# Gates' one-hots with two tokens side by side, eight tokens a step, in a two-layer transformer kernel

## The chip, the cores and the metric

The kernel runs on one core of a Trainium2 chip. The core has TensorE (PE: matmuls, and PEld: its weight loads), VectorE (DVE), ScalarE (ACT), GpSimd (POOL) and SyncE (SP), on whose queue the DMA transfers of this kernel are issued. The metric is the device time of one execution in microseconds; lower is better.

## The reference, cut to what matters

Two blocks of a transformer over 256 tokens of width 1024, in float32. Each block has a token mixer and ends with product-key experts (PEER); between the two comes cross attention to a memory. The change lies in the experts' part, which runs twice, once for each block:

```python
q = (xt @ w_pq).reshape(T, PEER_HEADS, 2, PEER_QDIM // 2)
s = jnp.einsum('thpd,hpnd->thpn', q, subkeys)          # 8 heads, 2 halves, 128 keys
top_s, top_i = lax.top_k(s, 16)
cand_s = top_s[:, :, 0, :, None] + top_s[:, :, 1, None, :]
best_s, best_pos = lax.top_k(cand_s, 16)               # over 256 candidates
expert = 128 * (first index) + (second index)          # one of 16384
gate = jax.nn.softmax(best_s, axis=-1)
act = jax.nn.gelu(jnp.einsum('thkd,td->thk', peer_u[eb], xb)) * gb
out = jnp.einsum('thk,thkd->td', act, peer_v[eb])
```

So each token selects 8 x 16 = 128 experts, each given by two indices from 0 to 127, and each has a gate.

## The kernel before, in words

The experts are not gathered. The kernel computes the first layer for all 16384 experts and all 256 tokens, multiplies by a dense table of gates that is zero where an expert was not selected, and multiplies by the whole second table. Every large float32 matmul is made of three of exact halves (`mm3`, line 292: high x high, high x low, low x high). A tile of weights, 128 x 1024, comes by DMA into one of four `raw` buffers; ScalarE rounds it to its high half `wh` and VectorE subtracts to get the low half `wl` (`split`, line 273; `weight`, line 282), each in two pieces of 512 columns, of which seven are held.

**The gates' table.** For one token t the table over first index i and second index j is a product of two one-hot matrices over the 128 selections: the sum over selections of gate x [second index = j] x [first index = i]. In `gates` (line 1141) this is done for four tokens at a time. `ids` holds the two indices of every selection (partition) and token in 16 bits, `gate` the gate times 2^15 in two 16-bit parts. VectorE makes `hot[:, 0:2]`, the one-hots of both indices (line 1148, 128 x 1024 elements: two indices, 128 values, four tokens), and then `hot[:, 2:4]`, the second one-hot times each part of the gate (line 1151, again 1024 elements). Both are in one `work` tile of 4 KB a partition; there are two, used by turns. TensorE then makes, for each token, two matmuls into the psum tile `pg` (line 1156): 128 stationary columns, a gate part's one-hot of that token, and 128 moving columns, the first index's one-hot of that token. As the token is the last axis of `hot`, these columns are taken with a step of four elements. ScalarE copies `pg` in two halves into `S` (line 1160), and after each 16 tokens two DMAs write `S` to the table `gd` in memory (line 1164). 256 tokens are 64 steps, and 512 `pg` matmuls in each of the two expert layers.

**What it is mixed with.** `up` (line 1169) is the first expert layer: for each of the 128 tiles of the table, a load, a split and 24 matmuls into `ph` (line 298) with 256 moving columns, and a gelu on ScalarE into `hid` after every second tile. `mix` (line 200) puts the steps of the selection and of the gates (`chain`, line 1216) between those of the table (at most 94 tiles, `AHEAD`) in one order: a tile of the table gives a credit of `UP` = 1.4, and each yield of the gates uses up `GATES` = 0.5 (after the one-hots) or 0.3 (after the copies). The order of the instructions on each engine is then settled by a scheduler on that order. Waits follow from the data. SP's queue has the loads and the writes in one order.

**What follows.** After the gates, `fetch` (line 1196) reads back the first part of the table, `gt`, `prep` (line 1201) multiplies it into `hid` on VectorE (line 1209) and splits the product into `dah` and `dal`, and TensorE begins the second layer, `acc` (line 1265), by turns with the rest of `up`. Large buffers come from a pool of 33 places of 4 KB a partition (`big`, `NBIG`): here four of the normalized input (`pxh`, `pxl`), four of scores (`S`), two `work`, and one of `hid` for four tiles of the table.

Of the kernel before, what the change touches and what calls it, by code (L numbers as in the profile page):

```python
# [27 lines left out]
# pairs (a, b) of ranks that can be among the 16 best sums of two descending lists of 16: (a + 1) * (b + 1) <= 16, in  # L28
# the order of a * 16 + b; runs of equal length: first a, how many, length
RUNS = [(0, 1, 16), (1, 1, 8), (2, 1, 5), (3, 1, 4), (4, 1, 3), (5, 3, 2), (8, 8, 1)]  # L30
NC = 50
# blocks of q (0-3), k and v of the gated delta rule, in the order of their use
# [3 lines left out]
# ---------------------------------------------------------------- host layout  # L36
def _cols(w):
    """[K, C] -> [C/128, 128 p, K/128, 128 c]: one stationary tile per 128 columns."""
    k, c = w.shape
    return np.ascontiguousarray(w.reshape(k // 128, 128, c // 128, 128).transpose(2, 1, 0, 3))  # L40


def _rows(w):
    """[K, 512] -> [K/256, 128 p, 2, 512]: moving tiles, two blocks of 128 rows each."""
    k, c = w.shape
    return np.ascontiguousarray(w.reshape(k // 256, 2, 128, c).transpose(0, 2, 1, 3))


def _vec(v):
    """[n*128] -> [128, n]"""  # L50
    return np.ascontiguousarray(v.reshape(-1, 128).T)
# [107 lines left out]
# ---------------------------------------------------------------- the program  # L159
class Vec:  # L160
    """[128, n, 256] kept as tiles of four blocks"""
# [8 lines left out]
class Blocks:  # L170
    """[128, 1024] kept as two halves; [k] is the k-th block of 128 columns"""
# [18 lines left out]
def weave(a, b):  # L190
    """steps of a and b by turns"""
    for _ in a:
        yield _
        v = next(b, None)
        if v is not None:
            yield v
    yield from b


def mix(a, b):  # L200
    """Two programs in one order. A step yields the vector engine's time that it takes, less what it leaves
    while the tensor engine is busy with it; a runs on what b leaves."""
# [16 lines left out]
class Norm:  # L219
    """x * g in exact halves (act), and the tokens' 1 / rms apart from it: rc with tokens on partitions, rb as rows.  # L220
    The latter are made when they are first asked for."""
# [12 lines left out]
class Net:  # L234
# [21 lines left out]
    # -- tiles  # L256
# [15 lines left out]
    # -- exact halves of float32: hi rounded to the tensor engine's float32r, lo the rest  # L272
# [9 lines left out]
    def weight(self, ap):  # L282
        """a tile [128, 1024] from memory: its exact parts, each as two halves"""
# [8 lines left out]
    def mm3(self, out, pairs):  # L292
        """sum of (ah+al)^T (bh+bl), without al^T bl, which is under float32's last place"""
# [7 lines left out]
    def dense(self, w, n, act, use):  # L301
        """w: tiles of 128 columns with K = 1024; use(pair, psum[128 c, 2 * 256 t])"""
# [11 lines left out]
    def dense_half(self, w, n, act, use):  # L314
        """w: tiles of two blocks of 128 columns with K = 512"""
# [10 lines left out]
    def dense_tok(self, w, act, use):  # L326
        """tokens on partitions: out[t, 512]; w: four moving tiles of two blocks of 128 rows; use(th, psum)"""
# [17 lines left out]
    def rsqrt(self, y, v, name):  # L345
        """y = v ** -0.5 for v > 0 on a few columns: a first value from the exponent, three Newton steps"""
# [14 lines left out]
    def spread(self, cols, n, out=None):  # L361
        """cols [128 t, n] -> the columns as rows on every partition: psum tiles of four [128, 128 t] each"""
# [12 lines left out]
    def begin(self, x, g, name, stats=True):  # L375
        """the norm of x[k] [128, 256] times g [128, 8], whose pairs of blocks are yet to be fed"""
# [51 lines left out]
    def colsum(self, ps, c, n, x):  # L428
        """ps[:, c] of n columns: the sums of x [128, 128 t] over its partitions"""
# [7 lines left out]
    def copies(self, v, N, scale=1.0):  # L437
        """use() that keeps pairs of column tiles in a Vec, times the tokens' 1 / rms"""
# [25 lines left out]
    def tables(self, which):  # L464
        """the activation tables that the calls of fn() after this one use, loaded after those before it are done"""
# [18 lines left out]
    # ------------------------------------------------------------ block 1, token mixer  # L484
    def sb_attention(self, qk, v, o):
        """stick-breaking; qk: Vec of 8 (4 of q / 8, 4 of k), two heads each; v [t][128, 512]; o: exact halves"""
# [4 lines left out]
        # scores, keys on partitions: of the first 128 keys all queries, of the others the last 128  # L491
# [17 lines left out]
        # softplus, which is zero where masked, and its sums over a key and those after it  # L509
# [24 lines left out]
    def gdn(self, pads, z, ba, out, ready):  # L534
        """gated delta rule; pads: 4 tiles [128, 3, 259] of q, k, v with three columns of zeros first;
        z [128 t, 2, 512]; ba [128 t, 2, 8] (b, then a); out: exact halves, Vecs of 4. ready: names of the blocks
        of pads, of ba and of z as they get there"""
# [17 lines left out]
        # beta, g, and the cumulative sums of g within chunks of 64  # L555
# [22 lines left out]
        gf = g.rearrange("p h c -> p (h c)")  # pack = 2 * head + half  # L578
# [13 lines left out]
        # l2 norms over the head's 128 partitions: k now, q with the output  # L592
# [18 lines left out]
        dm = self.big("dm", (8, 128))   # exp(gc_i - gc_j), i on partitions  # L611
        dt = self.big("dt", (8, 128))   # the same with j on partitions
        eg = self.big("eg", (8, 128))   # exp(gc) on every partition
# [8 lines left out]
        # of the differences d = gc_free - gc_partition only the signs that a causal pair can have  # L622
# [8 lines left out]
        # A, and q k^T with m on partitions  # L631
# [13 lines left out]
        # (I + A)^-1 by blocks of doubling size; Tm the inverse, P its transpose  # L645
# [11 lines left out]
        for s in (2, 4, 8, 16, 32):  # L657
# [25 lines left out]
            if s == 2:  # L683
                # meanwhile k and v with tokens on partitions, and q exp(gc)
# [14 lines left out]
        # u [c, dv] and w^T [dk, c]  # L699
# [11 lines left out]
        # the scan over chunks  # L711
# [38 lines left out]
    def head_out(self, po, th, z, g, out, rq=None, half=False):  # L750
        """the exact halves of rmsnorm(po * rq) * z * g for the heads' [128 t, 128], transposed; half: with z / 2"""
# [31 lines left out]
    def branches(self, gates, wa, oa, wb, ob, wout, N):  # L783
        """N: the norm of the new x.  x += (sigmoid(ga) * (oa @ wa) + sigmoid(gb) * (ob @ wb)) @ wout; gates: Vec of 16;
        sigmoid(y) = (tanh(y / 2) + 1) / 2"""
# [27 lines left out]
    def add_x(self, N):  # L813
        """use() that adds to x and feeds x's next norm"""
# [75 lines left out]
    # ------------------------------------------------------------ cross attention  # L890
# [23 lines left out]
    def patterns(self):  # L914
        """constants of the experts' selection, in 16 bits, which hold them"""
        nc = self.nc
        self.iota4 = self.sm("iota4", 512, F16).rearrange("p (i t) -> p i t", t=4)
        nc.vector.tensor_copy(self.iota4, self.c("iota").unsqueeze(2).broadcast_to([128, 128, 4]))
# [5 lines left out]
    def cross(self, N, kv):  # L924
# [54 lines left out]
        # the values of the last two heads, while the tensor engine has little else to do  # L979
# [10 lines left out]
    # ------------------------------------------------------------ product-key experts  # L990
    def peer(self, N, g, wpq, sub, shared, u, v, gelu, final):
        """returns psum tiles acc[t half][d half] of [128 t, 512] with x plus the experts' sums, and the tile of the
        final gain in rows"""
# [13 lines left out]
        # scores of half the heads and half the tokens each; later the gates on their way to memory  # L1007
# [133 lines left out]
        def gates():  # L1141
            for t0 in range(0, T, 4):
# [19 lines left out]
                if t0 % 16 == 12:  # L1162
                    for i in range(2):
                        nc.sync.dma_start(gd[t0 // 16, :, 64 * i:64 * i + 64, :], gs[i])
# [403 lines left out]
```

## Time and profile before

| | us |
|---|---|
| median of 3 runs | 2252.29 |
| lowest and highest run | 2251.95, 2252.83 |
| span of the profiled execution, first to last instruction | 2251.2 |
| VectorE busy in it | 1643.0 |
| ScalarE busy in it | 1229.7 |

Of the profiled execution the span is what the profile gives as its own time. The views below come from this one execution. In a view of groups a line is: line of the kernel, engine, operation, output<-input, shapes, xcount | busy us, mean ns of one | idle time of the engine just before them, and what ended it. Where a view gives instructions in order of time, neighbours of one line are drawn together; then the second number is the time from the first one's start to the last one's end. Matmuls are pipelined, so a matmul's duration is longer than the step from one to the next.

### The profile page before, as it was taken

The numbers are of one execution on the slowest core, as the hardware profiler recorded it, in microseconds if no ns is written. First come the engines' busy times: TensorE is split into PE (matmuls) and PEld (weight loads), VectorE is DVE, ScalarE is ACT, GpSimd is POOL, SyncE is SP. The second block draws the span as 40 slices with busy tenths as digits, with TensorE's granted clock in tenths as the row PEclk, the third lists the DMA queues.
The fourth block names the chain that finished last, engine by engine and source line by source line (L and its number), as shares of the span: only waits on it lengthen the run. The fifth ranks groups of instructions, "written<-read, shape, count | busy, mean of one in ns | idle before, by whom it ended". The sixth has DMA issues, their size and how long they took to land.

```text
span 2251.2 us, 40741 instructions
## 1 busy us (share of the span) xinstructions
PE 2230.4 (99%) x15268; PEld 2035.2 (90%) x15268; DVE 1643.0 (73%) x3568; ACT 1229.7 (55%) x2237; POOL 1.8 (0%) x12
## 2 busy tenths in 40 slices
PE   8999999999999999999999999999999999999998
PEld 8899899999999999888887899999999999988886
DVE  8776776989778656687446668998887765598544
ACT  6463455656555555565446545655655555566443
POOL 0000000000000000000000000000000000000000
PEclk9999999999999999999999999999999999999999
DMA  6442445455666767787555445455566766698653
GB/s 232 139 150 85 132 150 178 161 189 178 208 231 216 243 206 221 232 288 251 188 188 189 143 132 186 156 192 186 202 217 213 247 216 207 214 297 262 200 190 125
DMA packets 178681, 441.14 MB, mean 196 GB/s; under 512 B 13602, under 2 KB 79266, under 8 KB 178484
## 3 DMA queue, kind: packets, MB, share of 16 engines
q1 hardware_dynamic: 177764, 437.11, 59.3%
q8 instruction: 120, 1.97, 0.4%
q10 hardware_dynamic: 720, 1.44, 0.2%
q14 instruction: 77, 0.63, 0.1%
HBM read 403.89 MB, written 34.60 MB: 195 GB/s over the span
## 4 chain that ended last, share of the span: by engine, by line
PE 95%; DVE 3%; ACT 1%; issue 1%; DMA 0%; ACTq 0%
PE ph L298 32%; PE acc L1265 32%; PE mm L298 17%; PE pg L1156 5%; PE mm L339 3%; DVE wl L275 1%; PE psc L1027 1%; ACT wh L274 0%; PE px L665 0%; PE pp L673 0%; PE cs L937 0%; PE pt L679 0%; PE cpo L963 0%; PE acc L1243 0%; PE spread L371 0%
## 5 line engine op out<-in xcount | busy, mean ns | idle before, releaser
L274 ACT ACTIVATE wh<-raw 128x512 fp32r<-128x512 f32 x1388 | 866.6, 630 | 853.5 <-PE ph L298 308.4
L275 DVE TENSOR_TENSOR wl<-raw,wh 128x512 fp32r<-128x512 f32 x1388 | 944.9, 688 | 483.4 <-ACT wh L274 477.2
L298 PE MATMUL ph<-pxh,wh 128*128 128x256 f32 x2048 | 579.4, 283 | 0.0
L298 PE MATMUL ph<-pxh,wl 128*128 128x256 f32 x2048 | 571.9, 279 | 0.0
L298 PE MATMUL ph<-pxl,wh 128*128 128x256 f32 x2048 | 571.4, 279 | 0.0
L1265 PE MATMUL acc<-wh,dah 128*128 128x512 f32 x1024 | 405.5, 396 | 0.0
L1265 PE MATMUL acc<-wh,dal 128*128 128x512 f32 x1024 | 405.0, 396 | 0.0
L1265 PE MATMUL acc<-wl,dah 128*128 128x512 f32 x1024 | 405.0, 396 | 0.0
L298 PEld LDWEIGHTS ph<-pxh,wh 128*128 128x128 f32 x2048 | 386.5, 189 | 3.1
L298 PEld LDWEIGHTS ph<-pxl,wh 128*128 128x128 f32 x2048 | 385.5, 188 | 3.2
L298 PEld LDWEIGHTS ph<-pxh,wl 128*128 128x128 f32 x2048 | 384.8, 188 | 0.0
L1265 PEld LDWEIGHTS acc<-wh,dal 128*128 128x128 f32 x1024 | 192.3, 188 | 46.6
L1265 PEld LDWEIGHTS acc<-wh,dah 128*128 128x128 f32 x1024 | 192.4, 188 | 43.0
L1265 PEld LDWEIGHTS acc<-wl,dah 128*128 128x128 f32 x1024 | 192.4, 188 | 42.9
L298 PE MATMUL mm<-xnh,wh 128*128 128x256 f32 x496 | 142.7, 288 | 8.9 <-ACT wh L274 8.1
L298 PE MATMUL mm<-xnh,wl 128*128 128x256 f32 x496 | 141.4, 285 | 0.0
L298 PE MATMUL mm<-xnl,wh 128*128 128x256 f32 x496 | 140.7, 284 | 0.0
L1156 PE MATMUL pg<-work 128*128 128x128 f16 x1024 | 133.3, 297 | 0.0
L1156 PEld LDWEIGHTS <-work 128*128 128x128 f16 x1024 | 110.3, 118 | 4.5
L1209 DVE TENSOR_TENSOR hid<-hid,gt 128x512 f32<-128x512 f32 x128 | 86.0, 688 | 35.9 <-DMA gt<-gd 35.2
L274 ACT ACTIVATE dah<-hid 128x512 fp32r<-128x512 f32 x128 | 76.3, 621 | 61.9 <-DVE hid L1209 60.9
L298 PEld LDWEIGHTS mm<-xnh,wh 128*128 128x128 f32 x496 | 95.2, 192 | 11.2 <-ACT wh L274 8.1
(443 smaller groups left out, 2825.7 us busy)
## 6 DMA issues: line engine op xcount, KB each, us to landing
raw<-in_u_dram SPq DMA_DIRECT2D x256, 512.0 KB, 3.6
raw<-in_v_dram SPq DMA_DIRECT2D x256, 512.0 KB, 3.9
gd<-S SPq DMA_DIRECT2D x64, 512.0 KB, 4.1
gt<-gd SPq DMA_DIRECT2D x64, 512.0 KB, 5.8
raw<-in_w_gate_dram SPq DMA_DIRECT2D x32, 512.0 KB, 3.5
raw<-in_w_pq_dram SPq DMA_DIRECT2D x32, 512.0 KB, 3.5
raw<-in_w_g_dram SPq DMA_DIRECT2D x12, 512.0 KB, 4.7
raw<-in_w_qk_dram SPq DMA_DIRECT2D x8, 512.0 KB, 3.5
```

Source lines behind the costliest of these rows:

```text
L274: self.nc.scalar.activation(hi, src, AF.Copy)
L275: self.nc.vector.tensor_tensor(lo, src, hi.bitcast(F32), ALU.subtract)
L298: self.nc.tensor.matmul(out, l, r, start=i == 0, stop=i == n - 1)
L339: nc.tensor.matmul(ps[th], l, r, start=k == 0 and j == 0, stop=k == 7 and j == 2)
L1027: nc.tensor.matmul(pz[:, p * 128:p * 128 + 128], qf[:, p * 256 + th * 128:p * 256 + th * 128 + 128], key(h, p), start=True, stop=True)
L1156: nc.tensor.matmul(pg[:, t * 128:t * 128 + 128], hot[:, c, :, t], hot[:, 0, :, t], start=c == 2, stop=c == 3)
L1209: tt(hv, hv, gv, ALU.mult)
L1265: nc.tensor.matmul(acc[th][dh], l[:, n, sl], r.half[dh], start=i0 + n == 0 and j == 0, stop=i0 + n == 127 and j == 2)
```

## The change

One-hots are made for eight tokens at a time, as four pairs (`b`) of two tokens (`t`), with the two tokens of a pair side by side: the layout is (pair, index, value, token in pair) where it was (index, value, token). `ids` is kept in that order, and `iota4` becomes `iota2`. The one-hots of both indices of eight tokens are one VectorE instruction on 2048 elements and fill a whole `work` tile; the products with the gate's parts are two instructions on 1024 elements each: the second part goes into half of a new tile, `hots`, taken once from the pool of large buffers, and the first part into the place of the second index's one-hot. The matmuls are the same in number and size; their columns are taken with a step of two elements. The eviction of each four tokens is as before. The yields are 0.5, 0.5, 0.3 and 0.3 for eight tokens, and the write to memory comes after the last of them. The other lines of the diff take away comments and docstrings, which leaves the line numbers nearly as they were.

```diff
     def patterns(self):
-        self.iota4 = self.sm("iota4", 512, F16).rearrange("p (i t) -> p i t", t=4)
-        nc.vector.tensor_copy(self.iota4, self.c("iota").unsqueeze(2).broadcast_to([128, 128, 4]))
+        self.iota2 = self.sm("iota2", 256, F16).rearrange("p (i t) -> p i t", t=2)
+        nc.vector.tensor_copy(self.iota2, self.c("iota").unsqueeze(2).broadcast_to([128, 128, 2]))
...
-        ids = self.sm("ids", 512, F16).rearrange("p (c t) -> p c t", c=2)
+        ids = self.sm("ids", 512, F16).rearrange("p (b c t) -> p b c t", c=2, t=2)
...
-                nc.vector.tensor_copy(ids[:, :, th * 128:th * 128 + 128],
-                                      pt[:, 0:256].rearrange("p (c t) -> p c t", c=2))
+                nc.vector.tensor_copy(ids[:, 64 * th:64 * th + 64].rearrange("p b c t -> p c b t"),
+                                      pt[:, 0:256].rearrange("p (c b t) -> p c b t", c=2, t=2))
...
         def gates():
-            for t0 in range(0, T, 4):
+            spare = self.big("hots").bitcast(F16).rearrange("p (n b i t) -> p n b i t", n=2, b=4, t=2)
+            for t0 in range(0, T, 8):
                 if t0 % 16 == 0:
                     gs = [st[t0 // 16 % 2, i].rearrange("p a t -> p (a t)").rearrange("p (i t) -> p i t", t=16)
                           for i in range(2)]
-                # one-hots of the first index; of the second, times each part of the gate
-                hot = work[t0 // 4 % 2].bitcast(F16).rearrange("p (c i t) -> p c i t", c=4, t=4)
-                tt(hot[:, 0:2], self.iota4.unsqueeze(1).broadcast_to([128, 2, 128, 4]),
-                   ids[:, :, t0:t0 + 4].unsqueeze(2).broadcast_to([128, 2, 128, 4]), ALU.is_equal)
+
+                hot = work[t0 // 8 % 2].bitcast(F16).rearrange("p (b c i t) -> p b c i t", b=4, c=2, t=2)
+                part = [hot[:, :, 1], spare[:, t0 // 8 % 2]]
+                tt(hot.rearrange("p b c i t -> p (b c) i t"), self.iota2.unsqueeze(1).broadcast_to([128, 8, 128, 2]),
+                   ids[:, t0 // 2:t0 // 2 + 4].rearrange("p b c t -> p (b c) t").unsqueeze(2).broadcast_to(
+                       [128, 8, 128, 2]), ALU.is_equal)
                 yield self.GATES[0]
-                tt(hot[:, 2:4], hot[:, 1:2].broadcast_to([128, 2, 128, 4]),
-                   gate[:, :, t0:t0 + 4].unsqueeze(2).broadcast_to([128, 2, 128, 4]), ALU.mult)
-                pg = self.ac("pg")
-                for t in range(4):
-                    for c in (2, 3):
-                        nc.tensor.matmul(pg[:, t * 128:t * 128 + 128], hot[:, c, :, t], hot[:, 0, :, t],
-                                         start=c == 2, stop=c == 3)
-                pv = pg.rearrange("p (t i) -> p i t", t=4)
-                for i in range(2):
-                    nc.scalar.activation(gs[i][:, :, t0 % 16:t0 % 16 + 4], pv[:, 64 * i:64 * i + 64, :], AF.Copy,
-                                         scale=1 / GATE)
-                if t0 % 16 == 12:
+                yield self.GATES[0]
+                for c in (1, 0):
+                    tt(part[c], hot[:, :, 1], gate[:, c, t0:t0 + 8].rearrange("p (b t) -> p b t", t=2).unsqueeze(
+                        2).broadcast_to([128, 4, 128, 2]), ALU.mult)
+                for q in range(2):
+                    pg = self.ac("pg")
+                    for t in range(4):
+                        b, e = 2 * q + t // 2, t % 2
+                        for c in range(2):
+                            nc.tensor.matmul(pg[:, t * 128:t * 128 + 128], part[c][:, b, :, e], hot[:, b, 0, :, e],
+                                             start=c == 0, stop=c == 1)
+                    pv = pg.rearrange("p (t i) -> p i t", t=4)
+                    s0 = t0 % 16 + 4 * q
+                    for i in range(2):
+                        nc.scalar.activation(gs[i][:, :, s0:s0 + 4], pv[:, 64 * i:64 * i + 64, :], AF.Copy,
+                                             scale=1 / GATE)
+                    yield self.GATES[1]
+                if t0 % 16 == 8:
                     for i in range(2):
                         nc.sync.dma_start(gd[t0 // 16, :, 64 * i:64 * i + 64, :], gs[i])
-                yield self.GATES[1]
```

## Rows read from the trace of the kernel before

**Rows 1.** The page, part 1: the span; busy us, share of the span, instructions.
```profile
span 2251.2 us, 40741 instructions
...
PE 2230.4 (99%) x15268; PEld 2035.2 (90%) x15268; DVE 1643.0 (73%) x3568; ACT 1229.7 (55%) x2237; POOL 1.8 (0%) x12
```

**Rows 2.** The page, part 4: the chain that ended last, by line, shares of the span.
```profile
PE ph L298 32%; PE acc L1265 32%; PE mm L298 17%; PE pg L1156 5%; PE mm L339 3%; DVE wl L275 1%; PE psc L1027 1%; ACT wh L274 0%; PE px L665 0%; PE pp L673 0%; PE cs L937 0%; PE pt L679 0%; PE cpo L963 0%; PE acc L1243 0%; PE spread L371 0%
```

**Rows 3.** Table by stretch (header line: the columns): both gates' stretches, a later one.
```profile
core 0: us, PE busy (x) PEld busy (x) DVE busy (x) ACT busy (x) POOL busy (x), PEclk, DMA share, GB/s
577.36:739.52 162.16, 162.16 (x1378) 159.88 (x1377) 128.53 (x198) 95.64 (x217) 0.00 (x0) 1.00 0.62 216
1609.20:1771.50 162.30, 162.30 (x1380) 160.00 (x1379) 128.70 (x198) 95.65 (x217) 0.00 (x0) 1.00 0.62 216
...
1900.00:2100.00 200.00, 200.00 (x1043) 169.41 (x1042) 151.47 (x241) 114.97 (x198) 0.00 (x0) 1.00 0.78 250
```

**Rows 4.** Groups of the first gates' stretch: shapes, xcount | busy us, mean ns | idle.
```profile
L298 PE MATMUL ph<-pxh,wh 128*128 128x256 f32 x288 | 83.8, 291 | 0.0
...
L1156 PE MATMUL pg<-work 128*128 128x128 f16 x512 | 66.6, 297 | 0.0
...
L275 DVE TENSOR_TENSOR wl<-raw,wh 128x512 fp32r<-128x512 f32 x74 | 51.3, 693 | 32.1 <-ACT wh L274 30.4
```

**Rows 5.** Instructions in order of time, one table tile into `pg`: start us, us, engine.
```profile
602.36 0.28 PE L298 MATMUL ph<-pxh,wl 128*128 128x256 f32 x1
...
602.71 0.28 PE L298 MATMUL ph<-pxh,wl 128*128 128x256 f32 x1
...
602.83 2.05 PE L1156 MATMUL pg<-work 128*128 128x128 f16 x16
...
604.59 0.21 PEld L298 LDWEIGHTS ph<-pxh,wh 128*128 128x128 f32 x1
```

**Rows 6.** The same view of TensorE, `acc` matmuls after the stretch.
```profile
764.81 0.39 PE L1265 MATMUL acc<-wh,dah 128*128 128x512 f32 x1
...
766.44 0.40 PE L1265 MATMUL acc<-wl,dah 128*128 128x512 f32 x1
```

**Rows 7.** Groups by form, whole span: two matmuls, then weight loads.
```profile
L1027 PE MATMUL psc<-sub,pq 128*128 128x128 f32 x128 | 17.2, 274 | 0.0
...
L937 PE MATMUL cs<-ckT,cxq 128*128 128x256 f32 x32 | 7.9, 389 | 0.0
...
L298 PEld LDWEIGHTS ph<-pxl,wh 128*128 128x128 f32 x2048 | 385.5, 188 | 3.2
...
L1156 PEld LDWEIGHTS <-work 128*128 128x128 f16 x1024 | 110.3, 118 | 4.5
...
L1438 PEld LDWEIGHTS glo<-gstate,gq 128*64 128x64 f32 x32 | 3.1, 135 | 2.6 <-issue 1.2 <-DVE gstate L1432 0.4
```

**Rows 8.** Instructions in order of time, TensorE: the scores of one head.
```profile
497.40 1.05 PE L1027 MATMUL psc<-sub,pq 128*128 128x128 f32 x8
```

**Rows 9.** Groups by form on VectorE, whole span.
```profile
L275 DVE TENSOR_TENSOR wl<-raw,wh 128x512 fp32r<-128x512 f32 x1388 | 944.9, 688 | 483.4 <-ACT wh L274 477.2 <-PE mm L298 1.0
...
L1151 DVE TENSOR_TENSOR work<-work,gate 128x1024 f16<-128x1024 f16 x128 | 83.5, 686 | 0.7
...
L1113 DVE TENSOR_TENSOR work<-work,tf 128x1024 bf16<-128x1024 bf16 x8 | 9.7, 1216 | 0.0
```

**Rows 10.** Waits in the first gates' stretch: us in total, times, longest us.
```profile
DVE wl L275 <- ACT wh L274: 30.4, 48, 0.7
...
SPq L279 <- DVE wl L275: 111.6, 37, 4.3
```

**Rows 11.** Instructions in order of time, where `acc` begins.
```profile
751.08 1.29 DVE L275 TENSOR_TENSOR dal<-hid,dah 128x512 fp32r<-128x512 f32 x2
...
753.62 0.40 PE L1265 MATMUL acc<-wh,dah 128*128 128x512 f32 x1
```

## The prediction

> **What bounds the kernel now.** I read the totals first: TensorE is busy for 2230.4 of 2251.2 us, VectorE for 1643.0 [rows 1]. A busy TensorE only says that its queue was never empty, so the chain of waits comes next: nearly all of it is matmuls, and the product of the one-hots, `pg`, has 5% of the span, about 113 us [rows 2]. So a microsecond saved off TensorE, where nothing else ends last, comes off the time, and one saved off VectorE doesn't. Third, the table by stage: in the gates' stretch of the first expert layer TensorE is busy all 162.16 us at a granted clock of 1.00 (2.4 GHz), VectorE for 128.53, ScalarE for 95.64, and the DMA share is 0.62 [rows 3]. The second layer's stretch is the same to 0.2 us [rows 3]. In this stretch 288/8 = 36 tiles of the expert table (24 `ph` matmuls each) lie between 37 runs of `pg` matmuls [rows 4], so there are 74 runs in the two layers.
>
> **What one pg matmul costs.** Sixteen of them span 2.05 us, of which the last one's own duration is 0.297; that leaves 1.753 us for 15 steps, 117 ns each [rows 4, 5]. A `ph` matmul with 256 moving columns also steps by 117 ns (602.36 to 602.71, three steps) [rows 5]. One with 512 columns steps by 1.63/7 = 233 ns [rows 6]. So 256 more columns cost 116 ns, 0.45 ns a column, and 128 columns should cost 58 ns. `pg` has 128 columns and costs twice that. What sets it apart is its layout: with four tokens side by side a token's values stand 8 bytes apart, while `ph` reads its 4-byte values in a row. My reading: the stream is limited by 8-byte pieces, of which `pg` uses two bytes and `ph` all eight. The durations agree: 297 ns for `pg` with 128 columns [rows 4], 0.28 us for `ph` with 256 [rows 5].
>
> **The change, part by part.**
>
> *The step in memory.* With two tokens side by side a token's values are 4 bytes apart, the step at which `ph` reads. I take the 58 ns of a `ph` column rate. The bounds: no gain, 117, and 53 (128 columns at 2.4 GHz, from the clock in [rows 3]). 1024 matmuls x (117 - 58) = 60.4 us less. At 53 it would be 65.5.
>
> *What the borders of the runs keep.* After a run the first `ph` matmul needs its own weights, whose load starts with the last `pg` matmul's stream (604.59, where 602.83 + 1.753 = 604.58 [rows 5]). A 128-column f32 load takes 188 ns and one of 64 columns 135, so 64 columns are 53 ns and 128 are 106, the rest being latency [rows 7]. Now that load hides beside 117 ns of streaming, afterwards beside 58 only. So each of 74 borders gives back up to 106 - 58, about 50 ns: 3.7 us. If the new order splits runs, there are up to 128: 6 us.
>
> *VectorE.* Before, four tokens take one one-hot and one product of 1024 elements each, 686 ns apiece. Afterwards eight take a one-hot of 2048 and two products of 1024. At 16 bits 1024 elements take as long (686) as 512 in f32 (688), so it handles two a cycle [rows 9]; 1024 more elements are then about 0.53 us and the one-hot 1.22. Eight tokens: 1.22 + 2 x 0.69 = 2.60 us against 2.74. Worth nothing by itself: it lies beside TensorE. But the cover gets thin. The stretch shrinks from 162 to about 134 us, and VectorE's 128.5 less some 4 of saved fixed cost is 93% of that. Where work comes in lumps of 2.6 us on an engine that is 93% full, and its `wl` waits for ScalarE (30.4 us now [rows 10]) have to shrink to almost nothing, some of it shows. Bounds: 0 and 10 us a layer; I take 3 a layer, 6 in all, nearer the lower since those waits are only as long as TensorE holds the weight buffers.
>
> *DMA.* The same bytes in 134 us are a share of 0.62 x 162/134 = 0.75; in a later stretch of 200 us TensorE is busy throughout at 0.78 [rows 3]. Nothing.
>
> *The gates' write to memory* moves past a yield: the planner may now put a table tile in between, whose load then stands ahead of the write in SP's queue. SP waits for a free `raw` buffer 37 times, up to 4.3 us [rows 10]. During the stretch nobody needs the write. At its end they do: write, fetch, product and split end with `dal` at 752.37, and TensorE takes up `acc` at 753.62 [rows 11], when the five tiles that cover this are done (14.1 us after the stretch's end at 739.52, at 24 x 0.117 = 2.81 a tile): 1.25 us of slack. Bounds: 0 and 4.3 - 1.25 = 3 us a layer; I take 0.5, 1 in all, as most of SP's waits are shorter (111.6/37 = 3.0) and the planner need not put a tile there.
>
> *The third buffer* takes one of 33 big places until the last product. With it, four of the normalized input, four of scores, two of work and 22 of hidden values fill all 33 when the 23rd hidden tile is wanted: at table tile 89 of the 94 allowed ahead, the last one before those five. That tile waits for a score buffer that the write before frees. Only ScalarE's gelu waits, behind it the next splits; it belongs to the same bound as the write. The second index's product in place needs no wait, since both products are VectorE's own, in order. The smaller iota and the four rearranged copies of `ids` are under 1 us.
>
> **The sum**, against the span: 2251.2 - 60.4 + 3.7 + 6 + 1 = 2201.5. The runs' median, 2252.3, stands 1.1 above this span, which I add: 2202.6, say 2203.
>
> **The rivals.**
>
> 1. *Another floor near the old one.* Score matmuls `psc` with 128 contiguous f32 columns step by (1.05 - 0.274)/7 = 111 ns [rows 7, 8]: no 128-column matmul in this trace goes faster. If that is a floor of loading weights or of issue, `pg` gains 1024 x 6 = 6 us: 2246. Against it: f32 streams at half the rate, as 256 columns last 389 ns against 274 for 128, 115 more [rows 7], so 111 is its own stream; and `pg`'s weight load is recorded with 118 ns where an f32 load has 188 [rows 7], hence much shorter than the 106 above. A floor in between, at 80 to 90, gives 2218 to 2228. The Trainium skill (TensorE: Matmul & The Clock Gate, section Back-to-back issue gap) states about 81 ns per matmul for sustained pairs of load and matmul at 128 columns; by that estimate the first term is 1024 x 36 = 37 us and the time 2226. The `ph` rows don't show such an extra. 16% for a floor between 80 and 111.
>
> 2. *The step costs nothing now.* Then 117 ns is something that two-byte operands have anyway, the product keeps its time and VectorE's savings are off the path: 2252. For it: no row shows 16-bit operands at another step. Against: the exact factor of two in columns. The Trainium skill (SBUF — State Buffer, the note on cachelines in section Door 1) says that two hits in each 16-byte line are enough for full rate, and calls a step of up to 8 bf16 values free; `pg` has two hits a line already, so by this rule the change gains nothing. The 117 ns for 128 columns disagree with it. 10%.
>
> 3. *VectorE becomes the bound: slower.* The gate's and the index's operand is now a run of two values (4 bytes) repeated along 128 indices, where it was four (8 bytes). If VectorE then takes one element a cycle, 1024 elements cost the 1216 ns of the `low` product, which reads such a repeated operand [rows 9], and 2048 about 2.28 us: 4.7 us for eight tokens, 32 x 4.7 = 150 us a layer. With 74 splits `wl` of 0.69 [rows 4], 51, that is 201 us; successive instructions overlap by some 0.08 each (the second of two starts before the first one's end), about 15, leaving 186 against 162 in the stretch: 24 us more a layer, 2300. It decides as soon as eight tokens take more than (134 - 51)/32 = 2.6 us back to back for the gain to shrink, and (162 - 51)/32 = 3.5 for a loss. Against: the f32 operand of that row is itself repeated 4 bytes by 4 bytes and loses nothing beyond its width, 1024 cycles and the fixed part. 10%.
>
> **How the numbers follow.** Forecast 62%: 2203, its own range 2190 (all runs at 53 ns, no stall) to 2222 (10 us stalls a layer). Rival 1 has 16% and spans 2218 to 2246, rival 2 10% at 2252, rival 3 10% at 2300; 2% for anything else. A range from 2190 to 2246 leaves out rivals 2 and 3, about 20%. About 0.2%, 4.5 us, is what a measurement of this kernel can tell from no change. Faster takes the forecast and nearly all of rival 1: 0.78; same is rival 2 and the edge of rival 1: 0.12; slower 0.10.
>
> **What would show it.** Right: `pg` matmuls stepping by 56 to 62 ns and lasting about 235, the one-hot of 2048 at 1.2 us, products still 0.69, TensorE busy through a gates' stretch of some 135 us, everything after it unchanged but earlier. Steps of 80 to 111 say rival 1, 117 rival 2. Products of 1.2 us with TensorE waiting for VectorE say rival 3. Steps near 58 with the stretch well over 140 us would mean that the mechanism held and the stalls were undersized.

## The result, and the profile after

The changed kernel takes 2196.84 us (median of 4 runs, 2193.87 to 2197.23); the kernel before, timed beside it on the same chip, 2252.56 (2251.95 to 2255.14). The ratio is 0.9749, with an interval of 0.9735 to 0.9762: 2.5% less. The profiled executions' spans are 2195.4 and 2251.2 us, 55.8 apart.

The page of the changed kernel, its totals and the beginning of its chain of waits by line:

```profile
span 2195.4 us, 40524 instructions
...
PE 2173.8 (99%) x15268; PEld 1979.0 (90%) x15268; DVE 1627.1 (74%) x3504; ACT 1217.0 (55%) x2237; POOL 1.8 (0%) x12
...
PE ph L298 33%; PE acc L1274 30%; PE mm L298 18%; PE mm L339 3%; PE pg L1164 3%; DVE wl L275 1%; DMA gt<-gd 1%; PE psc L1027 1%; DVE dal L275 0%; PE px L665 0%; ACT wh L274 0%; PE pp L673 0%; DVE hid L1218 0%; PE cs L937 0%; PE pt L679 0%
```

Against [rows 1, 2]: the same 15268 matmuls keep TensorE busy for 56.6 us less, and `pg` falls from 5% of the span to 3%. TensorE is still the engine that sets the end. One small thing is new on the chain: the reading of the gates' table, `gt`, with 1%.

In order of time, from the last table matmul before a run of `pg` to the second one behind it (of the `pg` matmuls only the ends of the run are shown; there are sixteen):

```profile
588.58 0.28 PE L298 MATMUL ph<-pxh,wh 128*128 128x256 f32 x1
...
588.70 0.23 PE L1164 MATMUL pg<-work 128*128 128x128 f16 x1
...
588.77 0.22 PE L1164 MATMUL pg<-work,hots 128*128 128x128 f16 x1
...
589.57 0.22 PE L1164 MATMUL pg<-work,hots 128*128 128x128 f16 x1
589.57 0.19 PEld L298 LDWEIGHTS ph<-pxl,wh 128*128 128x128 f32 x1
589.60 0.36 PE L298 MATMUL ph<-pxl,wh 128*128 128x256 f32 x1
...
589.80 0.28 PE L298 MATMUL ph<-pxh,wl 128*128 128x256 f32 x1
```

Fifteen steps from 588.70 to 589.57 are 58 ns each, where they were 117 [rows 5], and a `pg` matmul lasts 0.22 us, where it lasted 0.297 [rows 4]. The next tile's first weight load starts with the last `pg` matmul, as before, and now has less to hide behind. The first `ph` matmul is drawn with 0.36 us and the second follows 0.20 us later, where inside a run of `ph` it is 0.28 and 0.117. That border was there before the change too:

```profile
604.63 0.37 PE L298 MATMUL ph<-pxh,wh 128*128 128x256 f32 x1
...
604.84 0.28 PE L298 MATMUL ph<-pxl,wh 128*128 128x256 f32 x1
```

From the start of the last `pg` matmul to the second `ph` it took 0.26 us then (604.58 to 604.84) and takes 0.23 now (589.57 to 589.80). The `pg` part of it has shrunk, the rest has grown.

The gates' stretch of the first layer up to the first `acc`, as a table by stretch, then only from the first to the last `pg` (columns: engine busy us and instructions, granted clock, DMA share, GB/s), and who waited in the longer of the two:

```profile
577.36:725.32 147.96, 147.96 (x1502) 146.41 (x1501) 130.34 (x182) 98.80 (x232) 0.00 (x0) 1.00 0.76 265
...
583.07:711.08 128.01, 128.01 (x1333) 126.51 (x1332) 116.99 (x162) 87.29 (x211) 0.00 (x0) 1.00 0.76 265
```
```profile
ACT wh L274 <- PE ph L298: 39.5, 68, 0.8
DVE wl L275 <- ACT wh L274: 15.2, 17, 1.7
```

TensorE is busy in every microsecond of both, at a granted clock of 1.00. VectorE is busy for 116.99 of 128.01 us, 91%, and its waits for ScalarE have fallen to 15.2 us in this stretch (30.4 in [rows 10]); no wait of TensorE for VectorE is recorded. A drawn matmul could hide a short one, but the steps show none either: from the first `pg` to the first `acc` the only steps of `ph` over 140 ns are the one behind each run of `pg`, before the change and after. `acc` begins at 725.32, where it began at 753.62 [rows 11]: 28.3 us of the 55.8 are won here. From there to the second layer's first `acc` the changed kernel wins another 29.8, 58.1 together.

The last 2.4 us are lost again in the second layer, behind its first `acc`. In order of time, VectorE and TensorE around 1998 us:

```profile
1997.98 0.69 DVE L1218 TENSOR_TENSOR hid<-hid,gt 128x512 f32<-128x512 f32 x1 [1.21 <-DMA gt<-gd]
...
1999.16 0.40 PE L1274 MATMUL acc<-wh,dah 128*128 128x512 f32 x1
1999.19 0.69 DVE L275 TENSOR_TENSOR wl<-raw,wh 128x512 fp32r<-128x512 f32 x1
...
1999.93 0.50 PE L1274 MATMUL acc<-wl,dah 128*128 128x512 f32 x1 [0.37 <-DVE wl L275]
```

Read it upwards: an `acc` matmul starts 0.77 us after the one before it instead of 0.23, since it waits for `wl`; `wl` stands on VectorE behind `hid` and a `dal`; and `hid` waited 1.21 us for the read of `gt`. Four more such steps, of 0.53 to 0.55 us, follow up to 2029 us.

### The profile page after: what moved, and what is told of

It is laid out like the page before. It is cut to its first block, busy times and chain, and to the rows that moved or that the text cites. A ratio compares the mean times of both kernels' runs of the same rounds, so it can differ in the third digit from the quotient of the medians.

```text
span 2195.4 us, 40524 instructions
## 1 busy us (share of the span) xinstructions
PE 2173.8 (99%) x15268; PEld 1979.0 (90%) x15268; DVE 1627.1 (74%) x3504; ACT 1217.0 (55%) x2237; POOL 1.8 (0%) x12
## 4 chain that ended last, share of the span: by engine, by line
PE 93%; DVE 4%; DMA 1%; ACT 1%; issue 1%; SPq 0%; ACTq 0%; DVEq 0%
PE ph L298 33%; PE acc L1274 30%; PE mm L298 18%; PE mm L339 3%; PE pg L1164 3%; DVE wl L275 1%; DMA gt<-gd 1%; PE psc L1027 1%; DVE dal L275 0%; PE px L665 0%; ACT wh L274 0%; PE pp L673 0%; DVE hid L1218 0%; PE cs L937 0%; PE pt L679 0%
## 5 line engine op out<-in xcount | busy, mean ns | idle before, releaser
L298 PEld LDWEIGHTS mm<-xnh,wl 128*128 128x128 f32 x496 | 95.5, 193 | 0.9 <-issue 0.6
L298 PEld LDWEIGHTS mm<-xnl,wh 128*128 128x128 f32 x496 | 95.8, 193 | 0.5 <-issue 0.3
```

The lines of the kernel that those rows point to most:

```text
L298: self.nc.tensor.matmul(out, l, r, start=i == 0, stop=i == n - 1)
```

## The experiments

**Theory.** The time comes from one thing, the step in memory at which the moving columns of `pg` are read: 8 bytes cost 117 ns per 128 columns, 4 bytes 58. Eight tokens at a time, the product in place, the third buffer and the new order are worth nothing. **Rivals.** The order and the larger instructions are what helps; or it is the stationary side, whose columns have the same step; or VectorE's cover has all but gone.

**1. All of the change but the pairs.** The changed kernel with four tokens side by side again, in two groups of four:

```diff
-        ids = self.sm("ids", 512, F16).rearrange("p (b c t) -> p b c t", c=2, t=2)
+        ids = self.sm("ids", 512, F16).rearrange("p (b c t) -> p b c t", c=2, t=4)
...
-                hot = work[t0 // 8 % 2].bitcast(F16).rearrange("p (b c i t) -> p b c i t", b=4, c=2, t=2)
+                hot = work[t0 // 8 % 2].bitcast(F16).rearrange("p (b c i t) -> p b c i t", b=2, c=2, t=4)
...
-                        b, e = 2 * q + t // 2, t % 2
+                        b, e = q, t
```

> The changed kernel with all of its new order (eight tokens a step, product in place, third buffer, same yields) but with four tokens side by side again, so that a column step is 8 bytes. Theory (the step in memory makes the gain): pg matmuls step by 117 ns and last 297 again, the time is 2250 to 2255 us, as before. Rival (the gain comes from fewer, larger VectorE instructions and the new order): pg steps by 58 or the time is near 2197 all the same. Both in part: between 2205 and 2245.

Measured: 2255.13 us (10 runs), ratio 1.0007 (0.9998 to 1.0017). Its groups by form:

```profile
L1164 PE MATMUL pg<-work,hots 128*128 128x128 f16 x512 | 125.4, 298 | 0.0
...
L1151 DVE TENSOR_TENSOR work<-iota,ids 128x2048 f16<-128x2048 f16 x64 | 78.4, 1225 | 34.6 <-PE pg L1164 34.6
```

The matmuls last 298 ns, as before the change. VectorE has time to spare, 34.6 us of waiting for `pg` to free its buffers. So order, size of the steps and buffer together are worth nothing that this interval can show.

**2. The pairs alone.** The kernel before, four tokens at a time and two `work` buffers, with only the layout in pairs (the product with the two parts of the gate then needs two instructions of 512 elements):

```diff
-                hot = work[t0 // 4 % 2].bitcast(F16).rearrange("p (c i t) -> p c i t", c=4, t=4)
+                whole = work[t0 // 4 % 2].bitcast(F16)
+                one = whole[:, 0:1024].rearrange("p (b c i t) -> p b c i t", b=2, c=2, t=2)
+                part = [whole[:, 1024 + 512 * c:1536 + 512 * c].rearrange("p (b i t) -> p b i t", b=2, t=2)
+                        for c in range(2)]
...
-                        nc.tensor.matmul(pg[:, t * 128:t * 128 + 128], hot[:, c, :, t], hot[:, 0, :, t],
-                                         start=c == 2, stop=c == 3)
+                        nc.tensor.matmul(pg[:, t * 128:t * 128 + 128], part[c][:, t // 2, :, t % 2],
+                                         one[:, t // 2, 0, :, t % 2], start=c == 0, stop=c == 1)
```

> The kernel before with pairs of tokens alone: four tokens a step, two work tiles, no third buffer, the write to memory where it was; the products of the two gate parts are two instructions of 512 elements. Theory: pg steps by 58 ns; VectorE has 0.61 + 2 x 0.34 = 1.29 us back to back for four tokens, 82 a layer, with the splits 127 a layer against 128 of TensorE, so 2195 to 2206 us. Rival (the larger step and the third buffer are needed, VectorE becomes the bound without them): TensorE waits for VectorE and the time is over 2210.

Measured: 2195.18 us (2194.11 to 2196.5), ratio 0.9742 (0.9724 to 0.976), which takes in the whole change. One run of sixteen `pg` matmuls, then its stretch up to `acc`:

```profile
584.17 1.09 PE L1161 MATMUL pg<-work 128*128 128x128 f16 x16
```
```profile
577.36:725.10 147.74, 147.74 (x1499) 146.16 (x1498) 134.97 (x274) 98.84 (x232) 0.00 (x0) 1.00 0.76 265
```

(1.09 - 0.22)/15 is 58 ns. VectorE has 4.6 us more to do than in the changed kernel (134.97 against 130.34), and TensorE is busy throughout all the same. The layout in pairs is the whole gain; eight tokens at a time only relieve an engine that nobody waits for.

**3 and 4. Moving and stationary columns apart.** The changed kernel with pairs for the first index (the moving columns) and fours for the second (the stationary ones), and the other way round:

```diff
-                hot = work[t0 // 8 % 2].bitcast(F16).rearrange("p (b c i t) -> p b c i t", b=4, c=2, t=2)
+                whole = work[t0 // 8 % 2].bitcast(F16)
+                first = whole[:, 0:1024].rearrange("p (b i t) -> p b i t", i=128, t=2)
+                second = whole[:, 1024:2048].rearrange("p (b i t) -> p b i t", i=128, t=4)
...
-                            nc.tensor.matmul(pg[:, t * 128:t * 128 + 128], part[c][:, b, :, e], hot[:, b, 0, :, e],
+                            nc.tensor.matmul(pg[:, t * 128:t * 128 + 128], part[c][:, n // 4, :, n % 4], first[:, n // 2, :, n % 2],
```

(In the other kernel `t=2` and `t=4` stand the other way round, and the divisors with them; in both the one-hots are two instructions of 1024 elements.)

> The changed kernel with the first index's one-hot (the moving columns) in pairs, 4 bytes a step, and the second index's one-hot and both products (the stationary columns) four side by side, 8 bytes a step; two one-hots of 1024 instead of one of 2048. If the moving stream is what the step in memory slows: pg steps by 58 ns, 2194 to 2203 us, weight loads of 118 ns. If the weight load is: 117 ns, 2250 to 2256. If each has a share: between, 80 to 100 ns.

> The other way round: moving columns four side by side (8 bytes a step), stationary ones in pairs (4 bytes a step). If the moving stream is slowed: pg steps by 117 ns, 2250 to 2256 us, weight loads of 97 ns. If the weight load is: 58 ns, 2194 to 2203.

Measured: 2201.34 and 2253.42 us (one run each). From both traces in order of time, two `pg` matmuls of a run, and the group of the weight loads; first moving pairs, then moving fours:

```profile
588.06 0.23 PE L1169 MATMUL pg<-work 128*128 128x128 f16 x1
...
588.84 0.22 PE L1169 MATMUL pg<-work,hots 128*128 128x128 f16 x1
...
L1169 PEld LDWEIGHTS <-hots 128*128 128x128 f16 x512 | 59.4, 116 | 0.0
```
```profile
590.80 0.30 PE L1169 MATMUL pg<-work 128*128 128x128 f16 x1
...
592.20 0.29 PE L1169 MATMUL pg<-work 128*128 128x128 f16 x1
...
L1169 PEld LDWEIGHTS <-hots 128*128 128x128 f16 x512 | 58.5, 114 | 0.3
```

Between the first pair of rows lie thirteen steps, 60 ns each; between the second twelve, 117 each. It is the moving columns' step that costs. The stationary columns' step matters little: with fours there, the two layers' runs of `pg` take 75.07 us in sum, where the changed kernel has 72.05. The rest of its distance of 4.5 us is no more than its waits of `acc` for `wl` explain, which are as at 1998 us above, but longer: the `acc` steps lose 5.6 us in this execution, and 2.4 in that of the changed kernel. The weight loads last 114 ns in the second kernel, where 97 was expected; the last section comes back to that.

**5. One token alone.** The changed kernel with each token's one-hot in a row (2 bytes a column). VectorE's repeated operand is then one value along 128 indices:

```diff
-                hot = work[t0 // 8 % 2].bitcast(F16).rearrange("p (b c i t) -> p b c i t", b=4, c=2, t=2)
+                hot = work[t0 // 8 % 2].bitcast(F16).rearrange("p (b c i) -> p b c i", b=8, c=2)
...
-                    tt(part[c], hot[:, :, 1], gate[:, c, t0:t0 + 8].rearrange("p (b t) -> p b t", t=2).unsqueeze(
-                        2).broadcast_to([128, 4, 128, 2]), ALU.mult)
+                    tt(part[c], hot[:, :, 1], gate[:, c, t0:t0 + 8].unsqueeze(2).broadcast_to([128, 8, 128]), ALU.mult)
```

> The changed kernel with each token's one-hot in a row by itself: columns step by 2 bytes, and the index's and gate's operands on VectorE are runs of a single value repeated along 128. Two theories of the stream: if it is limited by bytes or 8-byte pieces alone, pg steps by 53 to 57 ns, hardly less than now; if 58 is a floor of weight loads or issue, 58. VectorE: if runs of one value keep two elements a cycle, products stay at 0.69 us and the time is 2190 to 2198 us; if they fall to one a cycle (my price for the third rival), the one-hot takes 2.3 and the products 1.2 us, 4.5 us back to back for eight tokens, TensorE waits for VectorE in the gates' stretch and the time is 2285 to 2310 us, slower than before the change although TensorE's products cost half.

Measured: 2294.01 us (one run). Its groups by form, two `pg` matmuls of a run, and its stretch up to 760 us with two shorter ones out of it:

```profile
L1151 DVE TENSOR_TENSOR work<-iota,ids 128x2048 f16<-128x2048 f16 x64 | 146.2, 2287 | 0.9 <-PE pg L1164 0.8
L1158 DVE TENSOR_TENSOR hots<-work,gate 128x1024 f16<-128x1024 f16 x64 | 77.8, 1220 | 0.0
...
L1164 PE MATMUL pg<-work 128*128 128x128 f16 x512 | 68.2, 227 | 26.4 <-DVE work L1158 26.2
```
```profile
593.48 0.22 PE L1164 MATMUL pg<-work,hots 128*128 128x128 f16 x1
...
594.26 0.22 PE L1164 MATMUL pg<-work,hots 128*128 128x128 f16 x1
```
```profile
577.40:760.00 182.60, 149.26 (x1381) 142.39 (x1380) 181.19 (x165) 92.21 (x216) 0.00 (x0) 0.94 0.53 190
...
640.00:650.00 10.00, 6.62 (x63) 5.97 (x62) 10.00 (x10) 4.04 (x9) 0.00 (x0) 1.00 0.57 210
650.00:660.00 10.00, 9.25 (x79) 8.80 (x76) 10.00 (x10) 5.06 (x13) 0.00 (x0) 0.83 0.39 127
```

On TensorE nothing more is to be had: fourteen steps of 56 ns against 58. On VectorE the operand of single values halves the rate: 1220 ns for 1024 elements against 691, and 2287 for 2048 against 1218, so that 1024 more elements cost 1067 ns against 527. VectorE becomes the bound, busy for 181.19 of 182.60 us, and TensorE waits. That costs a little clock as well: after 10 us in which TensorE was busy for 6.62 its granted clock in the next 10 is 0.83, so a part of them ran at 1.2 GHz, not 2.4; over the stretch it is 0.94. This is my rival 3, at another layout: 2294 where I had put 2300. Two values side by side are the only layout of the three that both engines take at full speed.

**6. How much room VectorE has.** The changed kernel with its one-hots made twice, the same values again:

```diff
-                tt(hot.rearrange("p b c i t -> p (b c) i t"), self.iota2.unsqueeze(1).broadcast_to([128, 8, 128, 2]),
-                   ids[:, t0 // 2:t0 // 2 + 4].rearrange("p b c t -> p (b c) t").unsqueeze(2).broadcast_to(
-                       [128, 8, 128, 2]), ALU.is_equal)
+                for _ in range(2):
+                    tt(hot.rearrange("p b c i t -> p (b c) i t"), self.iota2.unsqueeze(1).broadcast_to([128, 8, 128, 2]),
+                       ids[:, t0 // 2:t0 // 2 + 4].rearrange("p b c t -> p (b c) t").unsqueeze(2).broadcast_to(
+                           [128, 8, 128, 2]), ALU.is_equal)
```

> The changed kernel with the one-hot instruction of each step issued twice (the second writes the same values): VectorE's work for eight tokens goes from 2.36 to 3.5 us back to back, nothing else changes. If VectorE's cover in the gates' stretch is thin, as predicted (93% busy): with the splits 32 x 3.5 + 35 x 1.22 = 155 us a layer against 128 of TensorE, so 20 to 27 us more a layer, 2237 to 2251 us. If VectorE has room (work done ahead of the stretch, waits that shrink): under 2215. If it is free: 2197.

Measured: 2229.85 us (one run), 33 more than the changed kernel, between the two cases that had been expected. Its stretch up to `acc` and two of its waits:

```profile
577.36:742.27 164.91, 154.03 (x1513) 147.91 (x1511) 157.92 (x211) 95.59 (x229) 0.00 (x0) 1.00 0.67 237
```
```profile
PEld ph L298 <- DVE wl L275: 11.4, 14, 0.8
PE ph L298 <- DVE wl L275: 9.0, 14, 0.6
```

The added work is 32 instructions a layer of about 1.14 us (1.22 less the 0.08 by which successive ones overlap), 36.5 us; the time grew by 16.5 a layer. So the changed kernel had about 20 us of room in each layer, close to the 147.96 - 130.34 = 17.6 us for which its VectorE is idle in the stretch. Experiment 5 agrees roughly (its clock is lower, too): there eight tokens take 2.1 us more, 68 a layer, and the time grew by 97/2 = 48.6. Dividing 20 by 32, an estimate is that eight tokens could have cost 0.6 us more before much of it showed; no run lies near that point.

**7 to 10. The late waits of `acc`.** The changed kernel again; the changed kernel with one more large place; the pairs alone (experiment 2) with one more large place; and the changed kernel with the reads of `gt` issued half a group of tiles earlier:

```diff
-NBIG = 33
+NBIG = 34
```
```diff
-            if i0 % 8 == 4 and i0 + 4 < 128:
+            if i0 % 8 == 0 and 40 <= i0 < 120:
+                fetch(i0 + 8)
+            if i0 % 8 == 4 and i0 + 4 < 48:
                 fetch(i0 + 4)
```

> The changed kernel itself once more, as the reference for the others on this chip: 2193.5 to 2197.5 us, pg steps of 58 ns. If the waits of acc in the second layer's later half belong to its order, they stand at the same place, 2 to 2.5 us; if they are chance, they are gone or elsewhere.

> The changed kernel with 34 large places instead of 33, which gives back the one that the third buffer takes. If the 2.4 us that TensorE loses in the second expert layer's later half come from that place (fetches of the gates' table wait for a free one): 2193.5 to 2195, no acc step over 0.4 us there, time 1.5 to 3 us under the changed kernel run beside it. If they come from the chance timing of transfers: within 1 us of it.

> Pairs of tokens alone (four tokens a step, no third buffer) with 34 large places. If neither the eight-token step nor the third buffer is worth anything, and the waits of the second layer's acc are chance: 2192 to 2196 us, within 2 us of the changed kernel. If four tokens a step leave VectorE too full: over 2200.

> The changed kernel with the gates' table fetched one half of a group (four rows, about 11 us) earlier in the second layer, from row 48 on. If the acc steps over 0.4 us behind the gates are VectorE's wait for a fetched part of the table, with the wl of a weight tile queued behind it: no such step, VectorE's waits for gt fall from 44 us to under 20, and the time is 2192 to 2195 us. If the waits have another cause: unchanged, 2195 to 2198.

(The last edit applies in both layers, not in the second alone.)

| kernel | median us (range) | ratio (interval) |
|---|---|---|
| changed, again | 2196.72 (2195.97 to 2198.34) | 0.9745 (0.9732 to 0.9758) |
| changed, 34 places | 2194.32 (2194.18 to 2196.06) | 0.9735 (0.9722 to 0.9749) |
| pairs alone, 34 places | 2194.31 (2194.05 to 2196.61) | 0.9741 (0.9728 to 0.9754) |
| changed, earlier reads | 2195.84 (2193.43 to 2199.94) | 0.9742 (0.9729 to 0.9755) |

The groups of `acc`'s weight loads by form show the waits for VectorE, first in the changed kernel, then with 34 places, then with earlier reads, then in the pairs alone of experiment 2:

```profile
L1274 PEld LDWEIGHTS acc<-wl,dah 128*128 128x128 f32 x1024 | 192.4, 188 | 46.0 <-DVE wl L275 3.4
```
```profile
L1274 PEld LDWEIGHTS acc<-wl,dah 128*128 128x128 f32 x1024 | 192.6, 188 | 44.2 <-DVE wl L275 1.5
```
```profile
L1276 PEld LDWEIGHTS acc<-wl,dah 128*128 128x128 f32 x1024 | 192.4, 188 | 46.8 <-DVE wl L275 3.9
```
```profile
L1270 PEld LDWEIGHTS acc<-wl,dah 128*128 128x128 f32 x1024 | 192.4, 188 | 43.0
```

The wait is there with 33 places (3.4 us, and 3.7 in the second execution, which has most of it in the first layer near 1020 us), less than half as long with 34, and absent in both kernels that make four tokens at a time. Reading earlier helped neither the wait (3.9 us) nor the time, and VectorE's waits for `gt` stayed at 41.7 us where under 20 had been expected.

With 34 places the median is 2.4 us lower than that of the changed kernel run beside it, and four of its five runs lie below all five of the other. That is what was expected if the third buffer's place is the cause. But the intervals of the ratios overlap, and of the 2.3 us between the two profiled executions only 1.3 lie in `acc`. The rest lies between the layers, around 1300 us, in a part that no version here touches. There the granted clock falls to 1.2 GHz for a while in every execution, as TensorE makes `pm`, matmuls of 128 columns 0.21 us apart, and it does not stay low equally long. The first layer's last `acc` and the second layer's first one are 544.9 to 545.7 us apart in the profiled executions of the change, the pairs alone and the change with 34 places and that of experiment 3, where the 20 us from 1295 have a granted clock of 0.83. They are 546.3 to 546.9 apart in those of the change again, the earlier reads and the pairs with 34 places, where it is 0.74. As a table by stretch, first the pairs alone, then with 34 places:

```profile
1295.00:1315.00 20.00, 20.00 (x126) 18.12 (x127) 7.21 (x12) 5.61 (x9) 0.00 (x0) 0.83 0.31 105
```
```profile
1295.00:1315.00 20.00, 20.00 (x112) 17.51 (x111) 6.55 (x11) 4.84 (x8) 0.00 (x0) 0.74 0.25 88
```

These two executions have spans of 2192.4 and 2194.8 us and neither has a wait of `acc` for `wl`: 2.0 of the 2.4 us lie there. What remains is that some 2 us are lost where VectorE waits for `gt`, at places that change between executions, and 1 to 2 us come and go with the clock. That the third buffer's place has a part in the first is likely, but not shown. No version here is better than the change by more than 0.2%.

## Why the prediction was right, and where it was off

2203 was forecast, 2196.84 measured; between the spans a gain of 49.7 us stood against one of 55.8.

- **The step in memory** (60.4 us, less 3.7 at the borders, 56.7): right in size, and in putting it on the step. The time from the first `pg` of a run to the second `ph` behind it, summed over all runs of both layers in the two traces, went from 130.28 to 72.05 us: 58.2. The step is 58 ns, and experiments 3 and 4 put nearly all of it on the moving columns. The reading behind it, a stream limited by 8-byte pieces, fits 117, 58 and 56 ns at steps of 8, 4 and 2 bytes. Another limit on the distance between columns would fit as well; no run tried a step between 4 and 8 bytes or above 8, so the reason for the halved rate is not shown.
- **The borders**: right in kind. From the last `pg` to the second `ph` a border now takes 230 ns, of which 58 + 117 are the two streams, so 55 are extra; before it was 255, 21 extra. A border gives back 34 ns, not 50, and there are 72 runs, not 74 (56 of sixteen matmuls and 16 of eight; the order didn't split them): 2.4 us for 3.7.
- **VectorE's stalls** (6 us, "some of it shows"): the step that failed. The load was right: one-hot 1.22 us, products 0.69, as forecast, and 91% busy between the first and the last `pg` where I had 93%. But the stalls are zero: TensorE is busy in each of the 128.01 us, and its steps hold no wait. I had taken a high busy share for a stall; a stall needs TensorE to run out of finished weights and one-hots, and no wait in the trace says that it did. I also read its idle time as used up; experiment 6 finds about 20 us of room a layer. From that I estimate the point at which more work shows as 2.36 + 0.6 = 3.0 us for eight tokens (2.36 being 1.22 + 2 x 0.69 less three overlaps of 0.08), not 2.6.
- **The write and the tail** (1 us): 14.2 us from the last `pg` to `acc` before and after, so nothing. The planner did move two tiles (5.71 us) ahead of the first `pg`; they are work that would have come anyway, and with them the stretch is 133.7 us, where some 135 was forecast.
- **Not in the sum**: 2.4 us of waits of `acc`, above. The sum had no term for anything after the stretch ("everything after it unchanged but earlier").

By differences: 1.5 us more from step and borders, 6 from stalls that did not come, 1 from the tail, 2.4 less from `acc`: 6.1, which is 55.8 - 49.7. That this closes to 0.1 us is luck. Counted matmul by matmul over the two executions, `pg` gives 57.5 us and `acc` takes back 2.4; in parts that the change does not touch `pm` took 2.0 less, since the clock fell later in it, and `mm` 1.5 more. That is 55.6 of the 55.8.

**The rivals.** Rival 1, another floor: the step of 58 ns with a weight load for each matmul leaves no floor between 80 and 111. Its prices were not on one footing: 2218 at 80 ns leaves out the 7 us of stalls and tail that 2226 at 81 has in it. The Trainium skill (TensorE: Matmul & The Clock Gate, section Back-to-back issue gap) gives some 81 ns for such pairs; this trace has 58 over runs of sixteen, so here the measurement decides against it. Rival 2, the step costs nothing: the 58 ns at 4 bytes refute it, and experiments 1 and 4 have 117 ns at 8 bytes whatever else is changed. The Trainium skill (SBUF — State Buffer, the note on cachelines in section Door 1) calls that step free for bf16 values, which have the size of these; for a moving operand of TensorE it costs half the rate in this kernel. Rival 3, VectorE falls to one element a cycle: the mechanism exists and its price was right (experiment 5), but it begins at runs of one value, not at runs of two.

## What to carry to other kernels

Divide the step between a kernel's matmuls by their columns and compare it with the other matmuls of the same trace. A group that takes twice the time per column may have its moving operand spread too far. It need not: `psc` takes 111 ns for 128 columns that lie in a row [rows 8]. So change the layout by itself, as in experiment 2; here it was worth all of the gain, and the order of the work nothing. When a layout is changed for one engine, cost it on the engine that writes it as well: at 2, 4 and 8 bytes a column this kernel took 2294, 2197 and 2255 us. And a busy share of 91% on an engine beside the bound is no stall yet; what tells is whether the bound ever waits for it. Last, where executions of one kernel differ by 1 or 2 us, compare the granted clock of the same stretch before looking for a cause in the change.

## What was not expected of the hardware

- The weights' step hardly counts. At 8 bytes the step of a `pg` matmul rises from 58 to 60 ns (experiment 3), while the same step of the moving columns doubles it. The recorded durations of the weight loads do not tell the two apart: 97 ns when both sides step by 4 bytes, 113 to 116 when only the weights step by 8, 114 when only the moving columns do. The duration of a load in the record is thus no measure of what it costs here.
- VectorE keeps its full rate for 16-bit elements with an operand that repeats two values 128 times, and takes about twice the time per element when it repeats a single value: 691 and 1220 ns for 1024 elements.
